# A fifth raw weight buffer, token forms at one address level, and a reordered hand-over between the blocks of a feed-forward layer

## The chip, the cores and the metric

One core of a Trainium2 chip runs the whole program once. The metric is the time of one execution in microseconds on the device. Five engines take part, each with its own queue in program order: PE (matrix products, with its weight loads listed apart as PEld), DVE and ACT (elementwise work), POOL, and SP, which issues most DMAs.

## The reference

A two-layer transformer on 512 tokens of width 1024, in float32. Four feed-forward (FFN) layers of inner width 2816 stand around two attention stages (`mla_mix`, `nsa_mix`). What matters here:

```python
def swiglu(x, w_gu, w_down):
    g, u = jnp.split(x @ w_gu, 2, axis=-1)
    return (jax.nn.silu(g) * u) @ w_down
...
    for layer in range(DEPTH):
        x = layer_norm(DN_ALPHA * x + 0.5 * swiglu(x, ffn_w_gu[layer, 0], ffn_w_down[layer, 0]), ...)
        ...                                   # attention, projection, layer_norm
        x = layer_norm(DN_ALPHA * x + 0.5 * swiglu(x, ffn_w_gu[layer, 1], ffn_w_down[layer, 1]), ...)
```

## The kernel before

Every float32 product is made of three products of rounded parts: a tensor is split into `hi` (a cast on ACT, L211) and `lo` (the rest, a subtraction on DVE, L212), and hi·hi, hi·lo and lo·hi are added in PSUM.

The inner width of an FFN layer is cut into 22 **blocks** of 128 features, in five **groups** (`GROUPS`). A letter `s` is a plain block; a letter `d` (77 of the 88) is made by a seven-product scheme: weights and tokens are each seen as two by two quarters (half of the 1024 inputs by gate and up, half of the inputs by half of the tokens), and seven products of combined quarters replace eight. The **token forms** `F.t[1]` to `F.t[4]` are the combined token quarters, made once for each layer by `token_forms`; the combined weights `g0` to `g3` are made for each block by `combined` (DVE, L154, L155, L160, L163) in the raw weight tiles themselves. One quarter product is `quarter`: 12 matmuls of 256 columns (L409 and L411 alternating, eight in all, then four of L415).

For a `d` block the helpers in `sevens` stand for the products: `m1` and `m2` (plain quarters `xhi`, `xlo`, into `r1`), `p7` (form 3, with g2), a product with form 2 (with g2, into `r2`), `p5` (form 1, with g1, into `r2`), a product with form 4 (with g1), and `p3` (the quarter 1,1, with g3, also into `r2`). `seeded` starts a new sum from the state of another one: ACT copies the PSUM half (L598); where the bank was not yet marked by a matmul, one matmul (L597) marks it. Between `p5` and `p3` DVE must have read `r2` for `us` (L620), since `p3` goes on adding to the same sum. The first block of a group makes the form-4 product first of all, into a bank of its own, and adds it on DVE later (L649, L650); the others seed it (L661). `m1` of the following block stands before `p5`, and `m2` of it before `p3`.

After a group's blocks follows its **down projection** `by_units` (the last group of a layer: `token_major`): for each weight unit `dn` and each of the four token tiles six matmuls of 512 columns (`prod`, L447 to L452), two tiles at a time; `residual` (DVE, L339) adds the result to `x` when a tile is done, which frees its two banks. There are eight PSUM banks, handed out in turn (`F.bk`).

Weights come by SP's queue into `wraw` (four tiles of 4 KB a partition), in the order of `_unit_order`; their hi and lo parts lie in seven pairs of ring tiles. `ahead(look)` prepares units up to `look` places ahead. A scheduler orders each engine's queue from the code's order, its priorities and the buffers that are free. The forms lie at fixed places: forms 1 to 3 in `F.fm`, form 4 behind an offset tile of 80 numbers. A copy `t5` of form 4 (made by two POOL DMAs in `second_t4`) lies behind an offset of 48 numbers; the first product of a group reads its first 128 rows from form 4 and the rest from `t5`, the later ones read `t5`. Read as byte addresses modulo 1024, `xhi`, `xlo` and forms 1 to 3 start at 192, form 4 at 512, `t5` at 704, and every weight tile at 768.

Of the kernel before, what the change touches and what calls it, by code (L numbers as in the profile page):

```python
# [9 lines left out]
F32 = mybir.dt.float32  # L10
# [19 lines left out]
DMA_RING = 4096  # L30
NCOLD = 16
NRAW, NRING, NEXTRA = 4, 3, 4
# [23 lines left out]
def _unit_order():  # L56
# [3 lines left out]
    def ffn(l, f, s):  # L60
        for m0, items in _groups(l, f):
            m = m0 + items.count("s")
            for i in range(m0, m):
                order.extend(("gu", (l, f, i, g), 1024, s) for g in range(2))
            end = m0 + len(items)
            for i in range(m, end):
                names = ("g0", "g1", "g2", "+", "g3") if i == m else ("g2", "+", "g1", "g3")
                for name in names:
                    if name != "+":
                        order.append((name, (l, f, i), 1024, s))  # L70
                    elif i + 1 < end:
                        order.append(("g0", (l, f, i + 1), 1024, s))
            m = end
            for i in range(m0, m):
                order.append(("dn", (l, f, i), 1024, s))
# [37 lines left out]
def tile_trunk(ctx: ExitStack, tc, a: dict, out):  # L113
# [173 lines left out]
    def open_f(scope):  # L287
# [11 lines left out]
        for i in (1, 2, 3, 0, 4):  # L299
            for e in "hl":  # L300
                if i:
                    F.fm.tile([P, 4, 256], F32, tag=f"t{i}{e}", name="place")
            if not i:
                F.fm.tile([P, 80], F32, name="offset")
# [170 lines left out]
    def by_units(names, lhs, on_tile, b, look):  # L475

        PS.set.update(range(8))

        n = len(names)
        tiles = [(b // 2 + i) % NT for i in range(NT)]  # L480
        ws = []
        for part in (tiles[:2], tiles[2:]):
            ps = {t: pair(t) for t in part}
            for k in range(n):
                if len(ws) == k:
                    ws.append(unit(*names[k], n - 1 - k))
                else:
                    ahead(look + k - n)
                for t in part:
                    prod(ps[t], ws[k], lhs(k, t), k == 0, k == n - 1)  # L490
                    if k == n - 1:
                        on_tile(t, ps[t])
# [51 lines left out]
    def ffn(l, f, i, halves, spill=None, final=False, mid=None, hook=None):  # L544
# [6 lines left out]
        tp.tile([P, 48], F32, name="offset")  # L551

        def second_t4():

            F.t[5] = [tp.tile([P, 4, 256], F32R, name=f"t5{e}") for e in "hl"]
            for t, s in zip(F.t[5], F.t[4]):
                nc.gpsimd.dma_start(t.bitcast(F32), s.bitcast(F32))

        for gi, (m0, items) in enumerate(groups):
# [4 lines left out]
            def fbank():  # L564
                F.bk += 1
                return bank(F.bk - 1)

            def evac(j, pg, pu, sg=None):
                sg = sg or hp.tile([P, T], F32, tag="sg", name="sg", bufs=3)
# [13 lines left out]
            def sevens(js):  # L583

                c0, c1 = slice(0, 256), slice(256, 512)
                op = nc.vector.tensor_tensor
                us, sg, w0, r1, r2 = {}, {}, {}, {}, {}

                def own():
                    PS.set.add(F.bk % 8)  # L590
                    return fbank()[:, c1]

                def seeded(src, w):
                    bits = F.bk % 8 in PS.set
                    r = own()
                    if not bits:
                        nc.tensor.matmul(r, lhsT=w[0][:, 0:P], rhs=F.xhi[:, 0, c0], start=True, stop=True)  # L597
                    nc.scalar.copy(r, src)  # L598
                    return r

                def m1(j):
                    if j not in w0:
                        w0[j] = unit("g0", (l, f, m0 + j), 4)
                    r1[j] = own()
                    quarter(r1[j], w0[j], 0, *quarters(0, 0))
                    r2[j] = seeded(r1[j], w0[j])

                def m2(j):
                    quarter(r1[j], w0[j], 512, *quarters(1, 0), start=False)
                    sg[j] = hp.tile([P, T], F32, tag="sg", name="sg", bufs=3)  # L610
                    nc.scalar.activation(sg[j][:, c0], r1[j], AF.Silu)

                def p7(j, w):
                    e = own()
                    quarter(e, w, 512, *F.t[3])
                    nc.scalar.copy(us[j][:, c0], e)

                def p5(j, w):
                    quarter(r2[j], w, 0, *F.t[1], start=False)
                    op(us[j][:, c1], us[j][:, c0], r2[j], op=ALU.add)  # L620

                def p3(j):
                    w = unit("g3", (l, f, m0 + j), 4)
                    quarter(r2[j], w, 0, *quarters(1, 1), start=False)
                    nc.scalar.activation(sg[j][:, c1], r2[j], AF.Silu)

                def finish(j):
                    g = sg[j]
                    nc.vector.scalar_tensor_tensor(g, g, 0.5, us[j], op0=ALU.mult, op1=ALU.mult)
                    split(hhi[:, j, :], hlo[:, j, :], g)  # L630

                for n, j in enumerate(js):
                    us[j] = hp.tile([P, T], F32, tag="sg", name="us", bufs=3)
                    following = js[n + 1] if n + 1 < len(js) else None
                    if n == 0:
                        w0[j] = unit("g0", (l, f, m0 + j), 4)
                        w = unit("g1", (l, f, m0 + j), 4)
# [3 lines left out]
                        ws = unit("g2", (l, f, m0 + j), 4)  # L641
                        p7(j, ws)
                        m2(j)
                        quarter(r2[j], ws, 0, *F.t[2], start=False)
                        nc.scalar.copy(sg[j][:, c1], r2[j])
                        if following is not None:
                            m1(following)
                        p5(j, w)
                        op(us[j][:, c0], us[j][:, c0], r3, op=ALU.add)  # L649
                        op(us[j][:, c0], us[j][:, c0], sg[j][:, c1], op=ALU.add)  # L650
                    else:
                        ws = unit("g2", (l, f, m0 + j), 4)
                        quarter(r2[j], ws, 0, *F.t[2], start=False)
                        r3 = seeded(r2[j], ws)
                        p7(j, ws)
                        if following is not None:
                            m1(following)
# [4 lines left out]
                    if following is not None:  # L662
                        m2(following)
# [1015 lines left out]
```

## Time and profile before

| | |
|---|---|
| median of 3 runs | 1864.7 us (1864.64 to 1865.83) |
| the profiled execution | 1864.2 us, of which the span of the profile 1862.5 us |
| PE busy | 1837.0 us (99% of the span), 12749 matmul records |
| DVE, ACT, POOL busy | 1346.2, 910.0, 170.0 us |
| DMA | 208.04 MB, the queues' mean share of the span 34% |

A busy time of PE is the union of its matmuls, which overlap: a matmul of 256 columns is shown as some 0.28 us long, yet the next one starts 0.113 or 0.118 us later. So the distance from start to start, not the busy share, tells how fast PE goes.

### The profile page before, as it was taken

To read this page: it belongs to the slowest core of one execution; us is meant where nothing else is said; L and a number is where in the kernel's file an instruction comes from. 1 tells how busy PE (TensorE), PEld (TensorE's weight loads), DVE (VectorE), ACT (ScalarE), POOL (GpSimd) and SP (SyncE) were. 2 spreads that over 40 slices of the span, in tenths; PEclk is the share of its full clock that TensorE was granted. 3 is DMA by queue.
4 is the path that set the end of the run, shared out by engine and by line. 5 is a ranking of instruction groups with operands and counts; after the bars stand their busy time and mean duration, and the time that the engine had idled before them with its cause. 6 is when DMAs were issued, how large, how long until landed. Compare 5 with 4: busy or idle time off the path is not lost. (4 is left out here: it accounts for less than half of the span.)

```text
span 1862.5 us, 31652 instructions
## 1 busy us (share of the span) xinstructions
PE 1837.0 (99%) x12749; PEld 1653.1 (89%) x12749; DVE 1346.2 (72%) x1999; ACT 910.0 (49%) x1671; POOL 170.0 (9%) x216
## 2 busy tenths in 40 slices
PE   9999999999999999999999999999999999999998
PEld 8899899996789899999899998999956699999987
DVE  8677687758668678677786876867667487767776
ACT  6345345456546335345653543544466354534533
POOL 0000000025500000000100000001266200000000
PEclk9999999999999999999999999999999999999999
DMA  7333334530235234134343423335321224323322
GB/s 266 111 114 99 117 113 138 184 114 24 68 114 170 69 113 131 63 114 147 114 156 104 135 71 111 125 101 172 108 52 28 112 89 140 114 68 125 124 69 80
DMA packets 61668, 208.04 MB, mean 112 GB/s; under 512 B 7152, under 2 KB 8320, under 8 KB 61520
## 3 DMA queue, kind: packets, MB, share of 16 engines
q1 hardware_dynamic: 57568, 194.46, 31.9%
q0 software_dynamic: 3520, 11.16, 1.8%
q8 instruction: 100, 1.64, 0.4%
q14 instruction: 48, 0.39, 0.1%
q10 hardware_dynamic: 432, 0.39, 0.1%
HBM read 188.16 MB, written 7.34 MB: 105 GB/s over the span
## 5 line engine op out<-in xcount | busy, mean ns | idle before, releaser
L211 ACT CAST whi<-wraw 128x1024 fp32r<-128x1024 f32 (+2 forms) x475 | 457.2, 975 | 526.0 <-PE bank L452 301.9
L212 DVE TENSOR_TENSOR wlo<-wraw,whi 128x1024 fp32r<-128x1024 f32 (+2 forms) x475 | 533.6, 1133 | 215.6 <-ACT whi L211 212.8
L409 PE MATMUL bank<-t,whi 128*128 128x256 f32 x956 | 232.6, 279 | 0.3 <-ACT bank L598 0.3
L411 PE MATMUL bank<-t,whi 128*128 128x256 f32 x956 | 232.5, 279 | 0.0
L409 PE MATMUL bank<-xhi,whi 128*128 128x256 f32 x924 | 226.2, 281 | 6.0 <-DVE us L620 4.7
L411 PE MATMUL bank<-xlo,whi 128*128 128x256 f32 x924 | 223.7, 278 | 0.0
L409 PEld LDWEIGHTS bank<-xhi,whi 128*128 128x128 f32 x924 | 174.0, 188 | 10.6 <-DVE us L620 8.4
L339 DVE SCALAR_TENSOR_TENSOR x<-x,bank 128x512 f32<-128x512 f32 x176 | 112.2, 683 | 96.4 <-PE bank L451 94.2
L409 PEld LDWEIGHTS bank<-t,whi 128*128 128x128 f32 x956 | 180.1, 188 | 1.2 <-ACT bank L598 0.5
L411 PEld LDWEIGHTS bank<-t,whi 128*128 128x128 f32 x956 | 180.0, 188 | 0.6
L411 PEld LDWEIGHTS bank<-xlo,whi 128*128 128x128 f32 x924 | 174.0, 188 | 0.0
L415 PE MATMUL bank<-t,wlo 128*128 128x256 f32 x940 | 146.7, 279 | 0.0
L415 PE MATMUL bank<-xhi,wlo 128*128 128x256 f32 x924 | 143.8, 278 | 0.0
L447 PE MATMUL bank<-whi,hhi 128*128 128x512 f32 x336 | 131.2, 390 | 0.0
L449 PE MATMUL bank<-wlo,hhi 128*128 128x512 f32 x336 | 131.0, 390 | 0.0
L448 PE MATMUL bank<-whi,hhi 128*128 128x512 f32 x336 | 130.9, 390 | 0.0
L450 PE MATMUL bank<-wlo,hhi 128*128 128x512 f32 x336 | 130.9, 390 | 0.0
L452 PE MATMUL bank<-whi,hlo 128*128 128x512 f32 x336 | 130.9, 389 | 0.0
L451 PE MATMUL bank<-whi,hlo 128*128 128x512 f32 x336 | 130.8, 389 | 0.0
L397 PE MATMUL bank<-xlo,whi 128*128 128x256 f32 x520 | 123.5, 279 | 2.3 <-DVE xlo L212 2.3
L415 PEld LDWEIGHTS bank<-t,wlo 128*128 128x128 f32 x940 | 125.7, 189 | 0.0
L395 PE MATMUL bank<-xhi,whi 128*128 128x256 f32 x520 | 124.7, 281 | 0.0
(346 smaller groups left out, 3786.1 us busy)
## 6 DMA issues: line engine op xcount, KB each, us to landing
wraw<-in_gu SPq DMA_DIRECT2D x173, 512.0 KB, 3.4
wraw<-in_dn SPq DMA_DIRECT2D x88, 512.0 KB, 3.6
wraw<-in_wo SPq DMA_DIRECT2D x16, 512.0 KB, 4.0
wraw<-in_wm SPq DMA_DIRECT2D x8, 512.0 KB, 4.3
x_dram<-x SPq DMA_DIRECT2D x8, 512.0 KB, 2.8
x<-x_dram SPq DMA_DIRECT2D x8, 512.0 KB, 4.4
wraw<-in_w SPq DMA_DIRECT2D x8, 512.0 KB, 3.6
wraw<-in_wq SPq DMA_DIRECT2D x6, 512.0 KB, 3.7
```

Of the source, the lines that this page charges most:

```text
L211: nc.scalar.copy(hi, src)
L212: return eng.tensor_tensor(lo, src, hi.bitcast(F32), op=ALU.subtract).ins
L395: nc.tensor.matmul(ps[:, c0:c1], lhsT=hi[:, k * P:(k + 1) * P], rhs=F.xhi[:, k, c0:c1], start=k == 0, stop=False)
L409: nc.tensor.matmul(ps, lhsT=hi[:, ks], rhs=(xh if k else fh)[:, k], start=start and k == 0, stop=False, skip_group_check=True)
L411: nc.tensor.matmul(ps, lhsT=hi[:, ks], rhs=(xl if k else fl)[:, k], start=False, stop=False, skip_group_check=True)
L415: nc.tensor.matmul(ps, lhsT=lo[:, ks], rhs=xh[:, k], start=False, stop=k == 3, skip_group_check=True)
L447: nc.tensor.matmul(p0, lhsT=ahi, rhs=hi[:, 0:512], start=first, stop=False)
L448: nc.tensor.matmul(p1, lhsT=ahi, rhs=hi[:, 512:1024], start=first, stop=False)
L449: nc.tensor.matmul(p0, lhsT=ahi, rhs=lo[:, 0:512], start=False, stop=False)
L450: nc.tensor.matmul(p1, lhsT=ahi, rhs=lo[:, 512:1024], start=False, stop=False)
L451: nc.tensor.matmul(p0, lhsT=alo, rhs=hi[:, 0:512], start=False, stop=last)
L452: nc.tensor.matmul(p1, lhsT=alo, rhs=hi[:, 512:1024], start=False, stop=last)
```

## The change

`NRAW` goes from 4 to 5 and the ring of software DMA descriptors from 4096 to 2048 bytes a partition. Form 4 moves to the level of the other forms (192); `t5`, its offset tile and its two copies go. A small tile `apart` (two times 128x256, behind an offset of 80 numbers, at level 512) takes a copy of the first 128 rows of form 3, by two POOL DMAs once for each layer.

All blocks now take the same products. The form-4 product is `p4`, seeded from `r2` after the form-2 product (`p6`) in every block, and stands between `p5` and `p3`. In a group's first block `p7` comes first, with `apart` in place of form 3's first rows.

The down projection becomes an object `ByUnits`. In the last block of a group (but the last of a layer), the weight unit of `dn`'s first block is prepared between `g2` and `g1`, the first of its token tiles (`early(0)`) is computed after `p7`, the second (`early(1)`) between `p4` and `p3`; `rest` makes the others and, ahead of the last unit of its second half, calls `between`, which is `m1` of the next group's first block. The scheduler's high priority is asked for the copies of `seeded` and `p7` on ACT and for the sum of `p5` on DVE. `sg` gets a fourth buffer.

```diff
-DMA_RING = 4096
+DMA_RING = 2048
-NRAW, NRING, NEXTRA = 4, 3, 4
+NRAW, NRING, NEXTRA = 5, 3, 4
...
             for i in range(m, end):
-                names = ("g0", "g1", "g2", "+", "g3") if i == m else ("g2", "+", "g1", "g3")
...
+                order.append(("g2", (l, f, i), 1024, s))
+                if i + 1 < end:
+                    order.append(("g0", (l, f, i + 1), 1024, s))
+                elif not last:
+                    order.append(dn.pop(0))
+                order.append(("g1", (l, f, i), 1024, s))
+                order.append(("g3", (l, f, i), 1024, s))
+            if not last:
+                dn.append(("g0", (l, f, end), 1024, s))
+            order.extend(dn)
...
+        def begin(self):
+            PS.set.update(range(8))
+            b = F.bk // 2
+            self.tiles = [(b + i) % NT for i in range(NT)]
+            self.ws.append(unit(*self.names[0], len(self.names) - 1))
+
+        def __call__(self, i):
+            t = self.tiles[i]
+            self.ps[t] = pair(t)
+            prod(self.ps[t], self.ws[0], self.lhs(0, t), True, False)
+
+        def rest(self, on_tile, look, between):
...
+                    if k == n - 1 and part[0] != self.tiles[0]:
+                        between()
...
-        tp.tile([P, 48], F32, name="offset")
+        tp.tile([P, 80], F32, name="offset")
+        apart = tp.tile([P, 2, 1, 256], F32R, name="apart")
...
+            with tc.high_priority():
+                nc.scalar.copy(r, src)
...
+        def p7(j, w, first=None):
+            e = own()
+            quarter(e, w, 512, *F.t[3], first)
+            with tc.high_priority():
+                nc.scalar.copy(us[j][:, c0], e)
+
+        def p5(j, w):
+            quarter(r2[j], w, 0, *F.t[1], start=False)
+            with tc.high_priority():
+                op(us[j][:, c1], us[j][:, c0], r2[j], op=ALU.add)
+
+        def p4(j, w):
+            quarter(r3[j], w, 512, *F.t[4], start=False)
+            op(us[j][:, c0], us[j][:, c0], r3[j], op=ALU.add)
...
-                        r3 = own()
-                        quarter(r3, w, 512, *F.t[5 if gi else 4], F.t[4])
-                        m1(j)
...
+                    if n:
+                        p6(j, ws)
+                        p7(j, ws)
+                    else:
+                        p7(j, ws, (apart[:, 0], apart[:, 1]))
+                        p6(j, ws)
                         m2(j)
...
+                    if following is not None:
+                        m1(following)
+                    elif not last:
+                        early.begin()
+                        early(0)
+                    w = unit("g1", (l, f, m0 + j), 4)
+                    p5(j, w)
+                    p4(j, w)
                     if following is not None:
                         m2(following)
+                    elif not last:
+                        early(1)
                     p3(j)
...
-                second_t4()
+                for e in range(2):
+                    nc.gpsimd.dma_start(apart[:, e].bitcast(F32), F.t[3][e][:, 0:1].bitcast(F32))
...
-                by_units(names, lhs, on_tile, F.bk, 4)
+                early.rest(on_tile, 4, lambda: m1(0, m0 + n))
```

**PE at the end of a group.** Before, the last block's form-4 product (its end is the row of `t5h`) is followed by a single matmul of the down projection and then by `p3` (the rows of `xhi` and `xlo`):

```order
L415 MATMUL bank<-t5h,wlo 128x256 x4
L447 MATMUL bank<-whi,hhi 128x512
L409 MATMUL bank<-xhi,whi 128x256
L411 MATMUL bank<-xlo,whi 128x256
```

In the changed kernel a whole token tile of the down projection stands there (`early(1)`):

```order
L417 MATMUL bank<-t,wlo 128x256 x4
L449 MATMUL bank<-whi,hhi 128x512
L450 MATMUL bank<-whi,hhi 128x512
L451 MATMUL bank<-wlo,hhi 128x512
L452 MATMUL bank<-wlo,hhi 128x512
L453 MATMUL bank<-whi,hlo 128x512
L454 MATMUL bank<-whi,hlo 128x512
L411 MATMUL bank<-xhi,whi 128x256
L413 MATMUL bank<-xlo,whi 128x256
```

So `p3` has moved five matmuls of 512 columns further from `p5` and `p4`.

**DVE at the start of a group.** Before, from the last two residual sums of the group before (`x2`) to the sum that `p3` of the group's first block waits for (L620), in the second group of the layer (0, 1):

```order
L339 SCALAR_TENSOR_TENSOR x2_5759<-x2_5759,bank_6819 128x512
L339 SCALAR_TENSOR_TENSOR x2_5759<-x2_5759,bank_6820 128x512
L212 TENSOR_TENSOR wlo_6960<-wraw_6957,whi_6959 128x1024
L212 TENSOR_TENSOR wlo_7005<-wraw_6919,whi_7004 128x1024
L154 TENSOR_TENSOR wraw_7076<-wraw_6957,wraw_7074 128x512
L155 TENSOR_TENSOR wraw_7074<-wraw_7074 128x512
L160 TENSOR_TENSOR wraw_7076<-wraw_7074,wraw_6957 128x512
L163 TENSOR_TENSOR wraw_6957<-wraw_6957,wraw_7076 128x512
L620 TENSOR_TENSOR us_6913<-us_6913,bank_6955 128x256
```

In the changed kernel, the same stretch:

```order
L341 SCALAR_TENSOR_TENSOR x2_5753<-x2_5753,bank_6817 128x512
L341 SCALAR_TENSOR_TENSOR x2_5753<-x2_5753,bank_6818 128x512
L217 TENSOR_TENSOR wlo_6981<-wraw_6978,whi_6980 128x1024
L160 TENSOR_TENSOR wraw_7065<-wraw_7065 128x512
L217 TENSOR_TENSOR wlo_7045<-wraw_6865,whi_7044 128x512
L165 TENSOR_TENSOR wraw_7067<-wraw_7065,wraw_6978 128x512
L168 TENSOR_TENSOR wraw_6978<-wraw_6978,wraw_7067 128x512
L217 TENSOR_TENSOR wlo_7000<-wraw_6926,whi_6999 128x1024
L618 TENSOR_TENSOR us_6925<-us_6925,bank_6905 128x256
```

The number of instructions ahead of the sum is the same; the first of the four weight combinations has moved ahead of the residual sums, and a half split (`wlo_7045`) has come in. On PE the sum's `p5` is now the group's fifth product and `p3` its eighth; before they were the seventh and the ninth.

More of the change, by code (lines that the diff above doesn't have):

```diff
@@ L60, in ffn @@
     def ffn(l, f, s):
[L61 to L62 removed]
+        groups = _groups(l, f)
+        for gi, (m0, items) in enumerate(groups):
+            end, m = m0 + len(items), m0 + items.count("s")
+            last = gi == len(groups) - 1
             for i in range(m0, m):
                 order.extend(("gu", (l, f, i, g), 1024, s) for g in range(2))
[L65 removed]
+            if gi == 0:
+                order.append(("g0", (l, f, m), 1024, s))
+            dn = [("dn", (l, f, i), 1024, s) for i in range(m0, end)]
             for i in range(m, end):
[L67 to L75 removed]
+                order.append(("g2", (l, f, i), 1024, s))
[8 more added lines that the diff above has]
+            order.extend(dn)
     ffn(0, 0, 0)
@@ L473, in token_major, with __init__ @@
         settle(1)
[L475 to L492, printed above, removed]
+    class ByUnits:
+        def __init__(self, names, lhs):
+            self.names, self.lhs, self.ws, self.ps = names, lhs, [], {}
+        def begin(self):
[8 more added lines that the diff above has]
+        def rest(self, on_tile, look, between):
+            n, ws, ps = len(self.names), self.ws, self.ps
+            for part in (self.tiles[:2], self.tiles[2:]):
+                for k in range(n):
+                    if part[0] == self.tiles[0] and k == 0:
+                        continue
+                    if k == n - 1 and part[0] != self.tiles[0]:
+                        between()
+                    if len(ws) == k:
+                        ws.append(unit(*self.names[k], n - 1 - k))
+                    else:
+                        ahead(look + k - n)
+                    for t in part:
+                        if t not in ps:
+                            ps[t] = pair(t)
+                        prod(ps[t], ws[k], self.lhs(k, t), k == 0, k == n - 1)
+                        if k == n - 1:
+                            on_tile(t, ps[t])
     def opening():
@@ new lines, in ffn, with fbank, own, seeded @@
+        op = nc.vector.tensor_tensor
+        us, sg, w0, r1, r2, r3 = {}, {}, {}, {}, {}, {}
+        def fbank():
+            F.bk += 1
+            return bank(F.bk - 1)
+        def own():
+            PS.set.add(F.bk % 8)
+            return fbank()[:, c1]
+        def seeded(src, w):
+            bits = F.bk % 8 in PS.set
+            r = own()
+            if not bits:
+                nc.tensor.matmul(r, lhsT=w[0][:, 0:P], rhs=F.xhi[:, 0, c0], start=True, stop=True)
+            with tc.high_priority():
+                nc.scalar.copy(r, src)
+            return r
@@ L559, in ffn, with p3, finish @@
+        def p3(j):
+            w = unit("g3", (l, f, m0 + j), 4)
+            quarter(r2[j], w, 0, *quarters(1, 1), start=False)
+            nc.scalar.activation(sg[j][:, c1], r2[j], AF.Silu)
+        def finish(j):
+            g = sg[j]
+            nc.vector.scalar_tensor_tensor(g, g, 0.5, us[j], op0=ALU.mult, op1=ALU.mult)
+            split(hhi[:, j, :], hlo[:, j, :], g)
         for gi, (m0, items) in enumerate(groups):
@@ L583, in sevens @@
             def sevens(js):
[L585 to L625, printed above, removed]
@@ L702, in ffn, with lhs @@
                     pass
-                second_t4()
+                for e in range(2):
+                    nc.gpsimd.dma_start(apart[:, e].bitcast(F32), F.t[3][e][:, 0:1].bitcast(F32))
+            names = [("dn", (l, f, m0 + j)) for j in range(n)]
+            def lhs(k, t):
+                return hhi[:, k, t * P:(t + 1) * P], hlo[:, k, t * P:(t + 1) * P]
+            early = ByUnits(names, lhs)
             sevens(range(j, n))
-            last = gi == len(groups) - 1
             if gi == 2 and mid is not None:
@@ L717, in on_tile @@
                     norm_tile(t, st, spill, final)
-            names = [("dn", (l, f, m0 + j)) for j in range(n)]
-            def lhs(k, t):
-                return hhi[:, k, t * P:(t + 1) * P], hlo[:, k, t * P:(t + 1) * P]
             if last:
```

62 lines of the change are left out of this document (22 added, 40 removed).

## The prediction

> **What bounds the kernel now.** I read the page first, then the waits, then PE's time stage by stage, and last the start times of single matmuls.
>
> ```profile
> span 1862.5 us, 31652 instructions
> PE 1837.0 (99%) x12749; PEld 1653.1 (89%) x12749; DVE 1346.2 (72%) x1999; ACT 910.0 (49%) x1671; POOL 170.0 (9%) x216
> PEclk9999999999999999999999999999999999999999
> ```
>
> PE is the bound, and its clock is full in every slice. Only what PE loses can be won. The next view takes the stages in which the seven products run: twenty windows, one a group, from the group's first quarter product to the end of its last `p3`. The columns are the window, its length, then busy time and count of PE, PEld, DVE, ACT and POOL, the clock and the DMA share. Eight of the twenty rows and the sum of all twenty:
>
> ```profile
> 40.50:61.30 20.80, 20.24 (x172) 19.89 (x171) 17.51 (x24) 12.64 (x20) 0.00 (x0) 1.00 0.62 199
> 150.00:199.80 49.80, 48.91 (x422) 48.48 (x421) 41.33 (x57) 29.70 (x50) 0.00 (x0) 1.00 0.46 152
> 287.60:327.00 39.40, 39.40 (x338) 39.28 (x337) 31.38 (x43) 22.97 (x39) 1.20 (x3) 1.00 0.48 157
> 634.70:674.40 39.70, 39.63 (x338) 39.29 (x337) 32.89 (x46) 22.95 (x39) 0.00 (x0) 1.00 0.40 134
> 696.00:745.40 49.40, 49.40 (x423) 49.28 (x422) 40.55 (x56) 28.07 (x48) 0.00 (x0) 1.00 0.42 137
> 968.90:999.70 30.80, 30.28 (x256) 29.95 (x256) 25.82 (x35) 18.26 (x30) 0.00 (x0) 1.00 0.50 171
> 1088.60:1136.70 48.10, 48.10 (x423) 47.85 (x422) 40.31 (x56) 28.37 (x48) 0.00 (x0) 1.00 0.45 141
> 1794.30:1832.50 38.20, 38.20 (x338) 38.18 (x337) 29.45 (x41) 20.70 (x36) 0.00 (x0) 1.00 0.30 97
> sum 760.30, PE 754.02 PEld 748.90 DVE 620.56 ACT 440.76 POOL 1.20; mean PE 37.70 PEld 37.45 DVE 31.03 ACT 22.04 POOL 0.06
> ```
>
> The five-block groups at 696 and 1088 do the same products, PE is busy all the time in both and the clock is 1.00, yet one takes 49.4 and the other 48.1 us. Single starts show why (second group of the layer (0, 1)):
>
> ```profile
> 634.50 0.39 PE L452 MATMUL bank<-whi,hlo 128*128 128x512 f32 x1
> 634.73 0.28 PE L409 MATMUL bank<-t,whi 128*128 128x256 f32 x1
> 636.11 0.28 PE L409 MATMUL bank<-xhi,whi 128*128 128x256 f32 x1
> ...
> 645.63 0.30 PE L409 MATMUL bank<-xhi,whi 128*128 128x256 f32 x1
> ...
> 647.06 0.28 PE L409 MATMUL bank<-t,whi 128*128 128x256 f32 x1
> ...
> 672.50 0.39 PE L447 MATMUL bank<-whi,hhi 128*128 128x512 f32 x1
> 672.96 0.39 PE L409 MATMUL bank<-xhi,whi 128*128 128x256 f32 x1
> ```
>
> From 636.11 to 645.63 stand seven products, 84 matmuls, in 9.52 us: 113.3 ns each. From 647.06 to 672.50 stand eighteen, 216 matmuls, in 25.44 us: 117.8 ns. The change of pace falls on the product at 645.63, the `p3` of the group's first block, which takes 1.43 us instead of 1.36, and it lasts until the next down projection. At 672.50 one matmul of 512 columns is followed only 0.46 us later, where 0.23 is its normal distance (634.50 to 634.73): the last block's `p3` waits. DVE at those two places:
>
> ```profile
> 641.03 1.23 DVE L212 TENSOR_TENSOR wlo<-wraw,whi 128x1024 fp32r<-128x1024 f32 x1 [2.98 <-ACT whi L211]
> ...
> 645.08 0.41 DVE L620 TENSOR_TENSOR us<-us,bank 128x256 f32<-128x256 f32 x1
> ...
> 671.89 0.68 DVE L212 TENSOR_TENSOR hlo<-sg,hhi 128x512 fp32r<-128x512 f32 x1
> 672.49 0.41 DVE L620 TENSOR_TENSOR us<-us,bank 128x256 f32<-128x256 f32 x1
> ```
>
> ```profile
> PEld bank L409 <- DVE us L620: 8.4, 12, 1.9
> L409 PEld LDWEIGHTS bank<-xhi,whi 128*128 128x128 f32 x924 | 174.0, 188 | 10.6 <-DVE us L620 8.4 <-ACT bank L598 1.5
> ```
>
> Both times `p3` stands behind the sum L620 by what is left of one product (1.36 us), and DVE reaches L620 late. So two losses: waits at L620, and the slower pace that a small wait can leave behind. Their size: 77 blocks of 7 products of 12 matmuls are 6,468; at 113.3 ns that is 733.0 us, and 17 of the windows hold one lone matmul of the down projection, 3.9 us. The windows sum to 760.3: 23.4 us are lost. PEld stands still for 760.3 - 748.9 = 11.4 of them; the other 12.0 are slow pace, about 2,670 matmuls at 4.5 ns. This bounds the gain.
>
> **The change part by part.**
>
> *The waits at L620.* In the changed order `p4` and `m2` (or `early(1)`) stand between `p5` and `p3` in every block but the last one of a layer's last group: two products, 2.72 us, for a sum of 0.41. In a group's first block DVE has, from the end of the down projection on, two residual sums, two whole splits, a half split and three combinations ahead of the sum:
>
> ```profile
> L212 DVE TENSOR_TENSOR wlo<-wraw,whi 128x1024 fp32r<-128x1024 f32 x387 | 471.6, 1228 | 205.1 <-ACT whi L211 203.2
> L339 DVE SCALAR_TENSOR_TENSOR x<-x,bank 128x512 f32<-128x512 f32 x176 | 112.2, 683 | 96.4 <-PE bank L451 94.2
> L163 DVE TENSOR_TENSOR wraw<-wraw 128x512 f32<-128x512 f32 x77 | 53.0, 689 | 1.4
> ```
>
> 2 x 0.683 + 2 x 1.228 + 4 x 0.69 = 6.6 us (a half split is priced as a combination), against five products, 6.8 us, until `p5` ends. The sum is then done 2.3 us ahead of `p3`. A whole block costs DVE 3 x 1.228 + 7 x 0.69 + 2 x 0.41 = 9.3 us against 9.52 of PE at the quick pace, so DVE keeps up, but barely; the row at 1088 shows that it does (quick pace, five blocks). The waits go. I keep 0.1 for each of the four last groups (39.40 - 39.28 in the row at 287), 0.8 for the first group at 968 (30.80 - 29.95: a copy of L598 comes late there, and `p6` will stand as near to it as `m2` did), 0.7 of the 1.3 at 150 (the splits of the memory input stay in the queues), 0.4 of the 0.9 at 40: 2.3 us, between 0 and 4.
>
> *The pace.* Without small waits the quick pace should hold from a group's start to its end, as at 1088 and 1794. But a switch from 512 to 256 columns can bring the slow pace by itself:
>
> ```profile
> 552.32 0.39 PE L384 MATMUL bank<-whi,mix 128*128 128x512 f32 x1
> 552.55 0.28 PE L395 MATMUL bank<-xhi,whi 128*128 128x256 f32 x1
> ...
> 553.73 0.28 PE L395 MATMUL bank<-xhi,whi 128*128 128x256 f32 x1
> ```
>
> No wait here (0.23 to the next), yet 10 matmuls take 1.18 us, 118 ns. That one enters with `xhi` at level 192. The group at 634.73, which enters with form 4 at level 512, takes 1.38 us for its first product and then 1.36. So the first rows' level seems to decide, and the changed kernel keeps such rows (`apart`, 512) at `p7` alone. It enters four products without them in each of 16 groups: `m1` inside the down projection, `p5` with `p4` behind `early(0)`, and `p3` behind `early(1)`. 48 matmuls x 4.5 ns x 16 = 3.5 us; at least 0, and if even `p7` fails, everything (below). Add 0.02 x 20 = 0.4 for the starts and 1.0 for one or two slips I don't foresee: 4.9 us of the 12.0 remain.
>
> [...]
>
> *Added on PE.* Two more switches from 256 to 512 columns in a group; after one, three matmuls take 0.69 instead of 0.68 us:
>
> ```profile
> 674.45 0.39 PE L448 MATMUL bank<-whi,hhi 128*128 128x512 f32 x1
> ...
> 675.14 0.39 PE L451 MATMUL bank<-whi,hlo 128*128 128x512 f32 x1
> ```
>
> 2 x 0.015 x 16 = 0.5. Four more marking matmuls, one in each layer's first group, 0.45. The products are as many as before. Together 0.95.
>
> *What lies beside other work.* DVE loses one sum of 0.41 a group, ACT a copy; neither is the bound. The fifth raw buffer and the earlier `dn` and `g0` loads act on weights that PE does not wait for; DVE waits for them (2.98 at 641.03 above, by way of ACT), and this cover is the room of 2.3 us. `apart` is a new thing to wait for in a layer's first group, on POOL's queue, where two copies of 512 KB go and two of 128 KB come:
>
> ```profile
> t5h<-t POOLq DMA_DIRECT2D x4, 512.0 KB, 5.5
> 963.52 2.36 DVE L212 TENSOR_TENSOR t<-wraw,t 128x1024 fp32r<-128x1024 f32 x2
> ```
>
> Form 3 is ready at 965.88 there, and `p7` comes one product after the stage's start at 968.9, at 970.4. Between 0 and 5.5 us of copying, the wait is 0 to 1; a quarter of the bytes is nearer to none, so I take 0. [...] The smaller descriptor ring: cost 0, since POOL's DMAs are needed microseconds after landing.
>
> *The sum.* 23.4 are lost now; 2.3 + 4.9 + 0.95 = 8.2 will be. Gain 15.2: the profiled execution's 1864.2 (1862.5 of span and 1.7 around it) goes to 1849.0. The median of the runs is 0.5 above that execution: 1849.5.
>
> **The rivals.**
>
> A. The waits go, the slow pace stays on as many matmuls, since something other than waits brings it. For it: in the row at 696 PEld stands still for only 0.12 us, and yet the group is 1.3 longer than the one at 1088. Against it: at 645.63 the change of pace falls on just the product that had waited. 2.3 + 12.0 + 0.95 = 15.3 lost, gain 8.1: 1856.5. [...]
>
> B. The inner entries run quick and the first groups' waits go too: 3.5 and 2.3 less than forecast, 1843.7.
>
> C. Slower: `apart` covers 128 rows and then steps back to level 192, where the old start stepped on to 704. If that fails to set the quick pace, all 6,468 matmuls take 4.5 ns more, 29.1 instead of 12.0: lost 29.1 + 2.3 + 0.95 = 32.4, that is 9.0 more than now: 1873.7. It decides from (23.4 - 3.3) / 0.0045 = 4,470 slow matmuls on. Against it: at 634.73, and in the row at 1088, a start at 512 was enough for the quick pace.
>
> D. The change doesn't do what it says: DVE's nearly full queue keeps L620 late, the wait only moves. Then the 8.4 us stay and most of the slow pace: 1862.5. Against it stand the 2.3 us of room.
>
> **How the numbers follow.** Forecast 0.57, A 0.16, B 0.10, C 0.07, D 0.10. A measurement of this kernel tells some 0.2%, 3.7 us, from no change. Below 1861 lie the forecast, A, B and a third of D: 0.86. Within 0.2%: the rest of D, 0.06; slower 0.08, C and what I have not seen. The range from 1843 to 1861 leaves out C, most of D and a little beyond B, under 2 in 10.
>
> **What would show it.** Right: the idle of PEld put down to the sum of `p5` falls from 8.4 to under 1 us; the twenty stages, counted without the down projection's matmuls, lose under 10 us to the quick pace; five-block groups take 113.3 ns a matmul behind `p7`, and `p5` after `early(0)` 118. Wrong: 117.8 ns from `p7` on (C), a new releaser of some us ahead of the lines of `quarter` (D), or a wait at `p7` for POOL's copy.

## The result, and the profile after

The changed kernel takes 1851.7 us, median of four runs (1846.1 to 1854.6), beside 1865.3 us for the kernel before (1864.6 to 1866.9): ratio 0.9922, 95% interval 0.9897 to 0.9947. The forecast was 1849.5. The profiled execution took 1853.0 us, 1851.3 of it span. In a second series it took 1850.4 us (experiment e5).

The page's first lines, to set beside those of before:

```profile
span 1851.3 us, 31666 instructions
PE 1831.2 (99%) x12753; PEld 1650.7 (89%) x12753; DVE 1346.2 (73%) x1979; ACT 914.9 (49%) x1671; POOL 170.3 (9%) x216
```

The same twenty stages of the changed kernel, three of the rows and the sum (columns as before). The windows are longer than before, since they now hold 384 matmuls of the down projection; so the two kernels are compared by what is lost in the windows, not by their lengths:

```profile
627.30:671.10 43.80, 43.80 (x362) 42.85 (x361) 35.38 (x47) 24.41 (x40) 0.00 (x0) 1.00 0.40 133
687.40:740.70 53.30, 53.30 (x446) 52.35 (x445) 44.06 (x58) 30.23 (x50) 0.00 (x0) 1.00 0.43 139
963.80:996.20 32.40, 32.21 (x269) 31.43 (x268) 25.43 (x33) 18.48 (x31) 0.00 (x0) 1.00 0.47 165
sum 828.50, PE 828.19 PEld 811.41 DVE 663.87 ACT 462.28 POOL 0.00; mean PE 41.41 PEld 40.57 DVE 33.19 ACT 23.11 POOL 0.00
```

6,468 matmuls of the products and 5 single ones (four marking ones, one lone) at 113.33 ns are 733.6 us, 384 of 512 columns at 226.7 are 87.0; so 828.5 - 820.6 = 7.9 us are lost, where 23.4 were. The waits for the sum went almost wholly. The first two rows are long waits outside the stages, the third is the sum's, and the last is the group of `p3`'s first rows:

```profile
PEld bank L399 <- DVE xlo L217: 2.5, 1, 2.5
PEld bank L384 <- ACT hT L216: 2.4, 1, 2.4
PEld bank L411 <- DVE us L618: 0.9, 3, 0.5
L411 PEld LDWEIGHTS bank<-xhi,whi 128*128 128x128 f32 x924 | 173.6, 188 | 2.4 <-DVE us L618 0.9
```

L620 had 8.4 us in 12 waits; its successor L618 has 0.9 in 3. The pace, in the second group of the layer (0, 1) again, by single starts (the first and the last of each product or stretch that the text measures):

```profile
627.28 0.28 PE L411 MATMUL bank<-xhi,whi 128*128 128x256 f32 x1
628.70 0.39 PE L449 MATMUL bank<-whi,hhi 128*128 128x512 f32 x1
...
631.41 0.28 PE L411 MATMUL bank<-apart,whi 128*128 128x256 f32 x1
632.80 0.28 PE L411 MATMUL bank<-t,whi 128*128 128x256 f32 x1
...
664.08 0.39 PE L449 MATMUL bank<-whi,hhi 128*128 128x512 f32 x1
665.46 0.28 PE L411 MATMUL bank<-t,whi 128*128 128x256 f32 x1
668.28 0.39 PE L449 MATMUL bank<-whi,hhi 128*128 128x512 f32 x1
669.64 0.28 PE L411 MATMUL bank<-xhi,whi 128*128 128x256 f32 x1
671.05 0.39 PE L449 MATMUL bank<-whi,hhi 128*128 128x512 f32 x1
```

`m1` inside the down projection: 1.42 us for twelve, 118 ns each. `p7` with `apart`: 1.39, and then 276 matmuls up to 664.08 in 31.28 us, 113.3 each. `p5` and `p4` behind `early(0)`: 2.82 us for 24, 117.5; `p3` behind `early(1)`: 1.41. Counted over all stages 1,152 matmuls are slow (5.3 us); 2,630 were before.

**What was not in the stages.** The stages won 23.3 - 7.8 = 15.5 us (by single starts), the span only 11.2. Clock and PE at the start of layer (1, 0) and in the projection ahead of it, in the changed kernel, then two rows of the kernel before at the same stall:

```profile
885.00:890.00 5.00, 2.71 (x15) 2.15 (x14) 4.56 (x6) 4.87 (x7) 2.97 (x4) 1.00 0.29 97
890.00:895.00 5.00, 5.00 (x32) 5.00 (x32) 4.81 (x8) 3.61 (x6) 0.00 (x0) 0.66 0.71 248
930.00:935.00 5.00, 2.84 (x23) 2.43 (x21) 3.54 (x6) 2.59 (x5) 0.00 (x0) 1.00 0.90 324
935.00:940.00 5.00, 4.97 (x23) 4.97 (x24) 4.45 (x7) 1.54 (x3) 0.00 (x0) 0.51 0.26 98
940.00:945.00 5.00, 5.00 (x38) 4.66 (x37) 2.73 (x5) 3.83 (x11) 0.00 (x0) 0.81 0.00 0
```

```profile
894.00:899.00 5.00, 2.71 (x15) 2.14 (x14) 4.56 (x6) 4.87 (x7) 2.98 (x4) 1.00 0.32 97
899.00:904.00 5.00, 5.00 (x45) 5.00 (x45) 4.94 (x8) 3.76 (x6) 0.00 (x0) 1.00 0.72 260
```

The stall of 2.5 us at 887 is in both kernels. Behind it the clock stayed at 1.00 before; after, it was 0.66 over 5 us (1.7 us lost). Behind the wait for `hT` at 933 it was 0.51 and 0.81 (3.4 us). That is 5.1 us, against 1.7 that the profile of before lost in the same way at 1360 to 1380 (0.95 and 0.88 over ten us each). The plain blocks make the rest: they change between the two paces by chance (e5). In three stretches of 213 to 285 matmuls, in the layers (0, 0), (0, 1) and (1, 1), 1, 243 and 32 were slow before, 216, 243 and 242 after: 425 more, 1.9 us; in the layer (1, 0) 239 were slow before and 16 after, 1.0 us less. 15.5 - 5.1 + 1.7 - 1.9 + 1.0 = 11.2, the span's gain. That it closes to the tenth is chance: the wait for `hT` itself grew too, from 1.3 to 2.4 us of PEld's time, and is not in this sum.

### The profile page after: what moved, and what is told of

Read it like the earlier page. It is cut to its first block, busy times and chain, and to the rows that moved or that the text cites. A ratio compares the mean times of both kernels' runs of the same rounds, so it can differ in the third digit from the quotient of the medians.

```text
span 1851.3 us, 31666 instructions
## 1 busy us (share of the span) xinstructions
PE 1831.2 (99%) x12753; PEld 1650.7 (89%) x12753; DVE 1346.2 (73%) x1979; ACT 914.9 (49%) x1671; POOL 170.3 (9%) x216
## 4 chain that ended last, share of the span: by engine, by line
PE 92%; DVE 4%; ACT 2%; issue 1%; DMA 1%; POOL 1%; POOLq 0%; DVEq 0%; ACTq 0%
PE bank L411 13%; PE bank L413 13%; PE bank L417 13%; PE bank L450 5%; PE bank L449 5%; PE bank L452 5%; PE bank L451 5%; PE bank L453 5%; PE bank L454 5%; PE bank L399 3%; PE bank L397 3%; PE bank L402 3%; PE tb L799 3%; PE o L827 2%; PE bank L386 2%; PE bank L384 2%
## 5 line engine op out<-in xcount | busy, mean ns | idle before, releaser
L411 PE MATMUL bank<-t,whi 128*128 128x256 f32 x1212 | 291.9, 277 | 0.0
L413 PE MATMUL bank<-t,whi 128*128 128x256 f32 x1212 | 291.6, 277 | 0.0
L413 PEld LDWEIGHTS bank<-t,whi 128*128 128x128 f32 x1212 | 227.8, 188 | 0.6
L411 PEld LDWEIGHTS bank<-t,whi 128*128 128x128 f32 x1212 | 227.7, 188 | 0.7
L411 PE MATMUL bank<-xhi,whi 128*128 128x256 f32 x924 | 223.0, 278 | 0.1
L417 PE MATMUL bank<-t,wlo 128*128 128x256 f32 x1232 | 190.6, 277 | 0.0
L417 PEld LDWEIGHTS bank<-t,wlo 128*128 128x128 f32 x1232 | 163.3, 188 | 0.0
L354 POOL TENSOR_TENSOR st<-st,cst 128x1 f32<-128x1 f32 x24 | 15.8, 659 | 1368.0 <-DVE st L353 1343.1
```

The lines of the kernel that those rows point to most:

```text
L411: nc.tensor.matmul(ps, lhsT=hi[:, ks], rhs=(xh if k else fh)[:, k], start=start and k == 0, stop=False, skip_group_check=True)
L413: nc.tensor.matmul(ps, lhsT=hi[:, ks], rhs=(xl if k else fl)[:, k], start=False, stop=False, skip_group_check=True)
L417: nc.tensor.matmul(ps, lhsT=lo[:, ks], rhs=xh[:, k], start=False, stop=k == 3, skip_group_check=True)
```

## Experiments

Each is the changed kernel with the edit shown; five runs or more each. Three chips were used (e1 to e4, e5 to e8, e9 to e12), so each time is set against the kernel before beside it, 1862.7, 1862.6 and 1864.5 us.

**e1: four raw buffers.**

```diff
-NRAW, NRING, NEXTRA = 5, 3, 4
+NRAW, NRING, NEXTRA = 4, 3, 4
```

> The changed kernel with four raw weight buffers instead of five; all else as changed. Theory: the fifth buffer isn't what took the waits away (the order of the products is), and it put one more weight cast ahead of hT on ACT, whose DMA lands late, in the stage ahead of layer (1, 0): PE waited 2.4 us there at 932 and the clock was down for some 7 us behind it. So PEld's wait for hT falls to about 1 us as before the change, the clock stays at 1.00 from 930 to 950, the twenty stages lose no more than 9 us to the quick pace (7.8 now), and the time is 1846 to 1850. Rival: DVE needs the fifth buffer; then waits of several us come back at L618 or at the weights of quarter, and the time is above 1853.

1855.6 us, ratio 0.9960 (0.9948 to 0.9972): some 5 us of the gain are gone. The waits of PEld, and the clock behind the first of them:

```profile
PEld bank L413 <- DMA apart<-t: 2.7, 1, 2.7
PEld bank L411 <- DVE us L618: 1.2, 3, 0.6
PEld bank L384 <- ACT hT L216: 0.7, 1, 0.7
```

```profile
960.00:965.00 5.00, 3.07 (x25) 2.71 (x24) 3.92 (x6) 1.66 (x2) 1.10 (x2) 1.00 0.42 136
965.00:970.00 5.00, 3.83 (x18) 3.84 (x19) 3.39 (x4) 2.50 (x5) 0.00 (x0) 0.55 0.41 143
```

The wait for `hT` was small, as the theory had it, but the time was the rival's, by a way neither had: `p7` of the layer (1, 0) waited for `apart`, and the clock fell. That stage alone lost 6.7 of the 13.4 us that the stages lost. At the sum of `p5` the fifth buffer shows too: in the groups' first blocks DVE began the sum 0.4 to 0.7 us behind the end of `p5`, as late as in the kernel before (0.64); in the changed kernel it begins 0.03 us behind it in most groups. With two products between `p5` and `p3` no wait came of it there.

**e2: p7 without `apart`.**

```diff
-                        p7(j, ws, (apart[:, 0], apart[:, 1]))
+                        p7(j, ws)
```

> The changed kernel whose p7 reads form 3 (level 192) from its first row on, without the copy at level 512 (the copies are still made). Theory: the level of the first rows read behind 512 columns sets the pace; then about 5,300 more matmuls of the seven products take 117.8 instead of 113.3 ns, 24 us, and the time is 1870 to 1878. Rival: only waits leave a slow pace behind; then nothing changes, 1848 to 1855.

1868.7 us, ratio 1.0039 (1.0027 to 1.0052): slower than the kernel before. One five-block group and the sum of the twenty windows:

```profile
694.20:749.10 54.90, 54.90 (x445) 53.96 (x444) 43.98 (x58) 30.26 (x50) 0.00 (x0) 1.00 0.40 134
sum 849.80, PE 848.29 PEld 832.09 DVE 668.18 ACT 464.27 POOL 0.00; mean PE 42.41 PEld 41.60 DVE 33.41 ACT 23.21 POOL 0.00
```

54.9 us instead of 53.3 in the group, 849.8 instead of 828.5 in all, and 5,975 slow matmuls. The edit changes nothing but where the first two matmuls of one product in a group read (DVE, ACT and POOL have as many instructions as in the changed kernel). So these two reads set the pace of a whole group: from the copy at level 512 it is quick, from form 3 at 192 it is slow. A copy at level 192 was not tried; that it is the level, and not the step from one tile to another, is not shown. All sixteen groups that follow a down projection are slow from end to end but for some 20 matmuls behind waits. Three of the four first groups, which follow plain blocks of their own width, had no more than 60 matmuls at 118 ns; so 4,820 more matmuls are slow than in the changed kernel, not the 5,300 that were expected, and the time lies below the expected range.

**e3: p4 ahead of p5.** The sum for the second half then holds the form-4 product too, which does not belong there, since `p4`'s sum is now added ahead of `p5`'s.

```diff
-                    p5(j, w)
-                    p4(j, w)
+                    p4(j, w)
+                    p5(j, w)
```

> The changed kernel with p4 ahead of p5, so that one product only (m2, or early(1)) stands between p5 and p3, as in the kernel before. Theory: the sum L618 is late again in a group's first block, p3 waits 0.1 to 1 us there in 8 to 16 groups, and a slow pace follows in most of them up to the down projection, about 1 us a group: 1858 to 1868. Rival: the shorter queue of DVE and the priority of the sum are enough by themselves: no waits, 1849 to 1855.

1854.3 us, ratio 0.9954 (0.9941 to 0.9967): in the rival's range, yet 5.3 us above e4 beside it. Waits come back, a half of what there was, but slow pace hardly (1,319 matmuls):

```profile
PEld bank L411 <- DVE us L618: 3.9, 8, 1.7
```

In this kernel the sum also follows an addition that it used to precede; e9 is the cleaner trial.

**e4: early(1) ahead of p5.**

```diff
+                    if following is None and not last:
+                        early(1)
                     p5(j, w)
                     p4(j, w)
                     if following is not None:
                         m2(following)
-                    elif not last:
-                        early(1)
                     p3(j)
```

> The changed kernel with early(1) ahead of p5, so that in a group's last block p3 stands one product (p4) behind p5. Theory: the waits at the end of the groups come back (8.4 us in all at L620 before, of which most stood at the ends of groups), 2 to 7 us, and no slow pace with them, since the down projection follows: 1854 to 1859. Rival: nothing comes back, since DVE now has one instruction less ahead of the sum: 1849 to 1854.

1849.0 us, ratio 0.9929 (0.9917 to 0.9941), the changed kernel's own ratio. L618 has 1.1 us in 3 waits; the theory fell. But the edit moves the token tile and doesn't take it away: both tiles of the down projection still stand ahead of `p3`, and so DVE still has their time to catch up (the traces are in the section on the prediction). Where the second tile stands makes no difference that can be seen here; what the two tiles are worth together was not tried.

**e5: the changed kernel again.**

> The changed kernel itself once more, as the measure for the three beside it, and to see what differs between two executions of one program. Theory: the seven products' stages lose the same 7 to 9 us to the quick pace every time, since their entries are set by the levels; what varies is the pace of the plain blocks (216 or 288 matmuls in a stretch, 1 us each, quick in one execution and slow in the next) and whether the clock drops behind the stalls of 2.4 us at the start of layer (1, 0) and ahead of it: 1847 to 1855, with the mean clock between 0.996 and 0.999. Rival: the spread comes from the waits of the stages themselves; then their losses differ from 7.8 us by several us.

1850.4 us (1846.2 to 1852.0), ratio 0.9930 (0.9918 to 0.9943). The stages lost 6.9 us, 1,114 slow matmuls; the three plain stretches held 216, 32 and 243 matmuls at 118 ns. Over the nine runs of this program the time goes with the mean clock: 1846.1 and 1846.2 us at 0.999, 1849.4 at 0.998, 1850.3 at 0.997, 1850.4 to 1854.6 at 0.996. The theory holds.

**e6: hT's products behind values(3).**

```diff
...
-        compressed(0, hb[0])
+        hT = transposed(0, hb[0])
         values(3)
-        compressed(1, hb[1])
+        compressed(0, hT)
+        compressed(1, transposed(1, hb[1]))
```

> The changed kernel with the transposes of hT ahead of the last quarter of the value product (values(3)) and the products with hT behind it, in the stage before layer (1, 0). Nothing else is changed. Theory: the fifth raw buffer put a third weight cast, which waits for its DMA, ahead of hT on ACT; with 24 matmuls in between PE doesn't wait for hT (1.3 to 2.4 us now), and there is no fall of the clock at that place: 2 to 6 us less than the changed kernel beside it. Rival: the stall moves to the next thing that waits for the same weights (the first products of the layer), and the time is the same within 1.5 us.

1847.5 us, ratio 0.9920 (0.9908 to 0.9933), 2.9 less than e5. PEld's wait for `hT` is 0.3 us, and the clock stays at 1.00 there, as the theory had it:

```profile
930.00:935.00 5.00, 4.86 (x43) 4.62 (x41) 4.79 (x10) 3.40 (x7) 0.00 (x0) 1.00 0.89 330
935.00:940.00 5.00, 4.63 (x40) 4.26 (x40) 4.94 (x8) 4.33 (x11) 0.00 (x0) 1.00 0.08 34
```

Why `hT` was late shows on ACT, in the changed kernel:

```profile
928.51 1.05 ACT L216 CAST whi<-wraw 128x1024 fp32r<-128x1024 f32 x1 [1.62 <-DMA wraw<-in_gu]
...
931.18 1.05 ACT L216 CAST whi<-wraw 128x1024 fp32r<-128x1024 f32 x1 [1.12 <-DMA wraw<-in_gu]
933.49 1.04 ACT L216 CAST whi<-wraw 128x1024 fp32r<-128x1024 f32 x1 [1.26 <-DMA wraw<-in_gu]
...
934.71 0.27 ACT L216 CAST hT<-bank 128x128 fp32r<-128x128 f32 x1
```

Three casts, each waiting for its own transfer, stand ahead of it; before it were two. But that the fifth buffer makes the stall fell with e10, which has four buffers, two casts, and 2.3 us of it. With four buffers it was 0.7 (e1) and 2.3 us, with five 0.8 (e9) to 2.4. The rows show the casts waiting for their transfers; what makes those land early or late was not tried.

**e7: no high priority** (the three `tc.high_priority()` in `seeded`, `p7` and `p5` are left out).

> The changed kernel without the high priority for the copies of seeded and p7 on ACT and for the sum of p5 on DVE. Theory: the priority moves the sum ahead of one or two weight combinations, and without it the sum is late again in some groups: the waits at L618 go from 0.9 to 3 to 8 us, those for the copies L590 to some us, and a slow pace follows in a part of the groups: 3 to 12 us more than the changed kernel beside it. Rival: the two products between p5 and p3 suffice: the same within 1.5 us.

1850.5 us, ratio 0.9934 (0.9922 to 0.9947): as e5. The sum's waits (L615 here) are 0.8 us in 3. The theory fell.

**e8 and e12: every entry at level 512** (the edits beside those of e6 and e4).

```diff
-                    if k == n - 1 and part[0] != self.tiles[0]:
-                        between()
...
+            between()
...
-                        p7(j, ws, (apart[:, 0], apart[:, 1]))
+                        p7(j, ws)
...
+                    p5(j, w, (inner[:, 0], inner[:, 1]) if entry else None)
...
-                early.rest(on_tile, 4, lambda: m1(0, m0 + n))
+                early.rest(on_tile, 4, lambda: m1(0, m0 + n, (apart[:, 0], apart[:, 1])))
...
-                    nc.gpsimd.dma_start(apart[:, e].bitcast(F32), F.t[3][e][:, 0:1].bitcast(F32))
+                    nc.gpsimd.dma_start(apart[:, e].bitcast(F32), quarters(0, 0)[e][:, 0:1].bitcast(F32))
+                    nc.gpsimd.dma_start(inner[:, e].bitcast(F32), F.t[1][e][:, 0:1].bitcast(F32))
```

> e6, and three edits to the entries of the seven products: early(1) stands ahead of p5, so that a group's last block has one switch from 512 to 256 columns instead of two; m1 of the next group stands behind the down projection instead of inside it; and the first rows of m1 at a group's start (from xhi, xlo) and of p5 behind early(1) (form 1) come from copies at level 512, while p7 reads form 3 from its first row on. The copy that m1 needs is ready long before, so nothing waits for the copy of form 3. Theory: every entry is then quick, and the slow matmuls of the twenty stages fall from 1,150 to under 300, 4 us, besides the wait for apart at layer (1, 0), 0.4 to 3: 4 to 7 us less than e6, and the slow ones that are left follow waits. Rival: m1 behind the down projection loses what it won inside it (its seeding or the weights of g0 come late, 0.2 to 0.5 us a group in 16 groups): 0 to 4 us more than e6.

1847.4 us, ratio 0.9924 (0.9910 to 0.9937); 196 slow matmuls in the stages, which lost 4.5 us. The pace came out as the theory had it; the time, which was to be 4 to 7 us under e6, is the same. So it was run again:

> e8 once more: its profile lost 4.7 us less in the stages than that of e6, but its median was the same. Theory: the 4 us are real and the executions of e8 fell on slow plain blocks and falls of the clock by chance; then this median is 2 to 5 us below that of e11 and the stages in the profile again hold under 300 slow matmuls. Rival: the pace of the stages varies between executions of e8 (its one profiled execution was also its fastest); then the median is that of e11 within 1.5 us, or the profile shows more slow matmuls.

1846.4 us, ratio 0.9910 (0.9889 to 0.9931), 4.8 less than e11 beside it. One five-block group and the sum (the windows hold 192 matmuls of 512 columns here):

```profile
688.40:738.80 50.40, 50.40 (x433) 49.89 (x432) 42.02 (x57) 29.11 (x49) 0.00 (x0) 1.00 0.42 136
sum 780.50, PE 779.33 PEld 770.79 DVE 634.02 ACT 446.89 POOL 0.00; mean PE 38.97 PEld 38.54 DVE 31.70 ACT 22.34 POOL 0.00
```

780.5 - 733.6 - 43.5 = 3.4 us lost, 165 slow matmuls. So the stages do as the theory says in both profiles: every entry that reads from a copy at 512 is quick behind its first matmuls, and `m1` needs no place inside the down projection. In the time the two series differ, level with e6 in one and 4.8 us under e11 in the other; both are 15 to 18 us under the kernel before, where the changed kernel is 12 to 14. It is the fastest version run, by a few us that its spread (1845.2 to 1850.5) nearly covers.

**e9: priority, last spacing and first spacing undone together.** Without high priority, early(1) ahead of p5, and in a group's first block:

```diff
+                    if n == 0:
+                        p4(j, w, False)
                     p5(j, w)
-                    p4(j, w)
+                    if n == 0:
+                        p4add(j)
+                    else:
+                        p4(j, w)
```

> The changed kernel without high priority, with early(1) ahead of p5 in a group's last block, and with p4 ahead of p5 in the first block (its sum on DVE stays behind that of p5): between p5 and p3 stands one product in the first and in the last block, as before. Theory: each cover alone was spare, together they are what ended the waits: 4 to 8 us at the sum of p5, and a slow pace behind a part of them; 1854 to 1862. Rival: what ended them is what is still there, the one sum less on DVE in a group's first block and the first weight combination made ahead of the residual sums: under 3 us of waits, 1848 to 1853.

1851.7 us, ratio 0.9933 (0.9913 to 0.9952): again the changed kernel's ratio, and the rival's range in time and waits. As in e4, both token tiles stay ahead of `p3`. **e10: the same with four raw buffers.**

> e9 with four raw weight buffers. Theory: without room between p5 and p3 DVE has no slack for weights that come a transfer later: 3 to 8 us more than e9, as waits at the sum and at the copies of seeded. Rival: four buffers cost what they cost alone (e1: 4 to 6 us over the changed kernel, of which the wait for the copy of form 3 and the fall of the clock behind it made 6.6 in the one stage at layer (1, 0)), or nothing.

1859.6 us, ratio 0.9972 (0.9959 to 0.9984), 8.0 more than e9, the theory's upper end. The sum's waits (L615 here) in e9, then in e10:

```profile
PEld bank L411 <- DVE us L615: 1.7, 3, 1.3
```

```profile
PEld bank L411 <- DVE us L615: 4.2, 6, 1.6
PEld bank L413 <- DMA apart<-t: 2.6, 1, 2.6
PEld bank L384 <- ACT hT L216: 2.3, 1, 2.3
```

The waits account for a part only. The mean clock of the two profiled executions was 0.995 in e10 and 0.998 in e9; over their spans of 1858.7 and 1850.1 us that is some 9 us lost against some 4. Among executions of the same mean clock (0.998, three of each) e10 takes 5.8 us more.

Of the 8.4 us at the sum, 4.2 are left in e10 and 1.7 in e9, so the fifth buffer takes some 2.5 of them. The changed kernel has 0.9, but the kernels with five buffers lie between 0.3 and 1.4 (e3 and e9 apart), so what spacing and priority add to the buffer can't be told from the spread of single profiles. What takes the first half stayed in every kernel: the sum that DVE no longer makes, the combination made ahead of the residual sums, `m1` ahead of the group, the two token tiles in a group's last block, and the fourth buffer of `sg`. They weren't tried apart.

**e11: e6, e4, and form 3 made ahead of form 4** (`form(3, v)` ahead of `form(4, u)` in `token_forms`).

> e6 with two more edits: form 3 is made ahead of form 4, so that the copy that p7 waits for in a layer's first group starts some 1.2 us or more earlier, and early(1) stands ahead of p5. Theory: the wait for apart at layer (1, 0), 0.7 us and the pace it leaves, goes, and the rest is as e6: 0.5 to 2 us less, 1845.5 to 1847. Rival: form 4 comes late for p4 instead, or nothing changes: 1847 to 1849.

1851.2 us, ratio 0.9927 (0.9908 to 0.9946). The time lies above both ranges that were given; by its ratio it is between e6 and the changed kernel. The wait for `apart` was 1.3 us, not less: the theory fell, and nothing is won here by the order of the forms.

## Why the prediction was right, and where not

The sum stood at 8.2 us lost in the stages; 7.9 were. By its parts:

- *The pace* (4.9 forecast, 5.3 measured). Entries behind 512 columns without rows at level 512 run slow: 48 matmuls a group were named, 51 or 52 were counted in most groups. That what the first two matmuls read decides is shown by e2, which does away with `apart`, and by e8 and e12, which extend it. One or two slips were allowed for; two groups, at 1606.9 and 1802.6, have one (waits of 0.09 and 0.16 us, then 118 ns to the group's end). In seven other places of the same profile waits of 0.11 to 0.46 us left the quick pace. So a wait can leave the slow pace behind, but only sometimes.
- *The waits and the switches* (3.3 forecast, 2.6 measured). The forecast worked them out at a group's first block: the sum was to be done 2.3 us ahead of `p3`, and it was done 2.1 us ahead in most groups, where before 0.14 us were left. The two products are more than that needs: in e9 and e10 one product is left between `p5` and `p3`, DVE takes up the sum 0.03 us behind `p5`, and it is done 0.74 us ahead. But all twelve of the waits that make up the 8.4 us stood somewhere else, at the groups' last blocks. There DVE came to the sum 0.8 to 2.7 us behind the end of `p5` (all groups but one), and `p3` had to wait. In the third group of the layer (0, 1), before, the end of `p5`, what DVE does first, the sum, and `p3`:

```profile
807.33 0.62 PE L415 MATMUL bank<-t,wlo 128*128 128x256 f32 x4
809.11 0.68 DVE L212 TENSOR_TENSOR hlo<-sg,hhi 128x512 fp32r<-128x512 f32 x1
809.71 0.42 DVE L620 TENSOR_TENSOR us<-us,bank 128x256 f32<-128x256 f32 x1
810.18 0.39 PE L409 MATMUL bank<-xhi,whi 128*128 128x256 f32 x1 [0.64 <-DVE us L620]
```

  The same place in the changed kernel, the end of `p5`, the sum and `p3`, and then the first two in e4:

```profile
801.54 0.64 PE L417 MATMUL bank<-t,wlo 128*128 128x256 f32 x4
803.03 0.41 DVE L618 TENSOR_TENSOR us<-us,bank 128x256 f32<-128x256 f32 x1
804.79 0.28 PE L411 MATMUL bank<-xhi,whi 128*128 128x256 f32 x1
```

```profile
802.25 0.63 PE L417 MATMUL bank<-t,wlo 128*128 128x256 f32 x4
802.92 0.42 DVE L618 TENSOR_TENSOR us<-us,bank 128x256 f32<-128x256 f32 x1 [0.46 <-PE bank L417]
```

  In the changed kernel DVE still begins the sum 0.85 us behind the end of `p5`, and `p4` with `early(1)`, 2.8 us, cover that. In e4 both tiles stand ahead of `p5`: DVE has caught up and itself waits for PE. So either place of the second tile ends the wait, and e4, e9 and e10, which keep both tiles ahead of `p3`, don't refute this cover. The traces fit the forecast's step here; a run without the tiles, which would show it, was not made.
- *The fifth buffer*, put at 0 with the room of 2.3 us as its cover, is the step that failed: with four buffers the time is 5 us longer in e1, and 8.0 longer in e10 than in e9. The loss lay for the most part not at the sum, where the 2.3 us of room were, but at `apart`: PE waited 3.5 us there in e1, against 0.4 in the changed kernel and at most 1.4 in any run with five buffers, and the clock fell behind it.
- *`apart`*, put at 0 out of 0 to 1, cost 0.4 us here. In the changed kernel, on DVE the second part of form 3, on PE the first two matmuls of `p7`, and the copies in the list of transfers (number, size, us from issue to landing):

```profile
960.00 1.22 DVE L217 TENSOR_TENSOR t<-wraw,t 128x1024 fp32r<-128x1024 f32 x1
```

```profile
965.29 0.28 PE L411 MATMUL bank<-apart,whi 128*128 128x256 f32 x1
965.76 0.39 PE L413 MATMUL bank<-apart,whi 128*128 128x256 f32 x1 [0.19 <-DMA apart<-t]
```

```profile
apart<-t POOLq DMA_DIRECT2D x8, 128.0 KB, 4.0
```

  A quarter of the bytes took 4.0 us where 512 KB took 5.5: nearer to the row than to nothing.
- *What lay outside the stages* was taken as unchanged. It moves by 4 us from run to run, and the profiled execution had the bad end of it: 4.3 us, which is the whole error against its own time (1853.0 for 1849.0).

So the number came out in part by luck: the pace and the cover of the sum were sized rightly, but by the same sum the change without its fifth buffer would have been forecast at the same time, and without it (e1) the kernel takes 5 us more.

Of the rivals, A (the pace stays: 1856.5) is refuted by the 1,152 slow matmuls, where 2,630 were before. B's condition, quick inner entries, came only with e8's edits. C, that the switch fails, is what e2 looks like: 1868.7. What D rests on, a late sum, stayed in the last blocks, but under the cover.

## What to carry to other kernels

Where PE is full, look at start-to-start distances, not at busy shares: 4% of pace (113.3 against 117.8 ns) hid behind 99% busy here, and where one product's first two matmuls read, behind a switch from 512 to 256 columns, set it for the next 276 matmuls in the group at 627 (quick behind `apart`, slow in e2). Before crediting a reordering with a gain, undo its parts together and not only one by one, and look in the trace whether the edit undid them: e4 moved a cover and left it in force, and the part that was priced at nothing cost 5 us when it was taken away. Price a stall of PE like those here, 1.6 to 2.7 us of PEld's time, with another 1.7 to 3.4 us as a risk: so much was lost to the clock behind them in some executions.

## What the runs showed of the hardware

- Back-to-back matmuls of 256 columns took one of two paces at full clock, 113.3 and 117.8 ns. PE held one or the other for hundreds of matmuls (276 quick ones from 632.80 on in the changed kernel, 216 slow ones from 647.06 on in the kernel before), and behind a wait of 0.09 us (at 1606.9 in the changed kernel) or first rows read from another place (e2) it went at the slow one. For the plain blocks it fell differently in executions of one program (216, 32, 243 slow in e5; 216, 243, 242 in the first profile).
- Waits of PE were followed by half clock in some executions and not in others: by 0.50 from 891 to 894 in the changed kernel, for some 3.4 us (0.66 over 5 us), and from 936 to 941.5, for twice that (0.51 and 0.81). Half clock also shows in the distances: from 891.00 to 892.28 in the changed kernel, and behind the wait for `apart` in e1, matmuls of 256 columns start 0.21 us apart. The wait of PE of 2.3 us that begins at 887.6 in the changed kernel stands in all fourteen profiles (2.5 us of PEld's time); behind it the clock was 0.66 over 5 us in the changed kernel and in e5, 0.67 in e2, 0.89 and 0.77 in e6, and 1.00 in the kernel before. A shorter one did it too: behind 1.6 us of PEld's time at `hT` the clock was 0.95 and 0.71 in e5, while it stayed at 1.00 behind 0.9 us at the same place in the kernel before.
